# Ten of the twelve modulation tensors of a two-layer diffusion trunk, computed on GpSimd instead of TensorE

## The chip, the cores and the metric

The kernel runs on one core of one Trainium2 chip. Its time is the device time in microseconds of one execution; lower is better. TensorE multiplies matrices into PSUM, VectorE (DVE) and ScalarE (ACT) do elementwise work, GpSimd (POOL) is a fourth compute engine that this kernel hardly uses, and SyncE (SP) issues all DMAs from one queue, in order.

## The reference, cut to what matters

Two layers are applied to 128 context tokens and 512 latent tokens, with the same weights for both kinds. Each layer needs six modulation vectors of 1024 numbers for each kind of token: a shift, a scale and a gate for the mixer half, and the same for the ConvFFN half.

```python
def adaln(cvec, w, b):                       # w: (1024, 6 * 1024)
    m = jax.nn.silu(cvec) @ w + b
    return m.reshape(cvec.shape[0], 6, D_MODEL)

def trunk_layer(x, mod, lp, cache):
    sh_m, sc_m, gt_m, sh_f, sc_f, gt_f = [mod[:, i][:, None] for i in range(6)]
    h = rmsnorm(x, lp['norm_g'][0]) * (1 + sc_m) + sh_m
    ...                                      # three branches: GQA attention, S5, neighbourhood attention
    x = x + gt_m * rmsnorm(merged @ lp['w_out'], lp['norm_g'][1])
    h = rmsnorm(x, lp['norm_g'][2]) * (1 + sc_f) + sh_f
    f = conv_ffn(h, ...)
    return x + gt_f * rmsnorm(f, lp['norm_g'][3])
```

So twelve vectors in all (two layers by six), each the product of a 2x1024 matrix (one row for the context tokens, one for the latent ones) with a 1024x1024 block of w_mod. All data are float32.

## The kernel before, in words

The dense weights come as 308 chunks of 128x1024 floats (512 KB), 154 for each layer, in the order of their use. `ws_next` hands out one chunk: at each call it prepares the chunks up to two ahead (`ws_prep`: ScalarE rounds the raw chunk to `hi`, VectorE takes `lo = raw - hi`; both through helpers, lines L130 and L99) and issues the loads up to four ahead (`ws_load`, which keeps the last issue as `last_ws`). There are two raw buffers and three pairs of hi and lo. A dense product is three TensorE passes (hi by hi, hi by lo, lo by hi; all matmuls have line L227). A chunk of the dense kind is 48 matmuls on 640 tokens, in halves of 384 and 256.

The order in a layer: S5 input projection (zu, 4 chunks), S5 sums and scan, GQA projections (zq 4 and zkv 2), gates, GQA attention, S5 output and GLU, branch products, then the neighbourhood attention with its projections (nv 4; nq and nk for each of four head pairs) woven with the rest of the gates and branch products, then w_out (8 chunks, one of them loaded twice), the FFN's up-projection (44 chunks; conv and SiLU on VectorE and ScalarE), and w_down (22 chunks for three token tiles, and then for the other two tiles in reverse, three of them kept, so 41 loads). In layer 0's up-projection the S5 bases and taps of layer 1 (`s5_pre`: many products on VectorE) are woven in, one step for each chunk. The order of instructions on each engine is made when the program is built, by a scheduler that follows program order as priority (`top()` raises it) and a simulated clock; each engine then runs its list in order, and so does the DMA queue of SP.

Modulation vectors 0 and 1 of layer 0 are computed in `setup`. The other ten are computed by `adaln` (L466): vectors 2, 3 and 4 of layer 0 in the neighbourhood stage (woven in at 1.4 steps for each step of that stage, with one raw buffer, into PSUM bank m1), vector 5 of layer 0 and all six of layer 1 in layer 0's up-projection (two raw buffers, bank tq). One step loads 512 KB of w_mod and does four matmuls of 256 columns, one on each 32-column quarter of the array, with the conditioning vectors (padded to 32 columns, tile `scv`) as the stationary side:

```python
for q in range(4):
    self.mm(acc[32 * q:32 * q + 32, 0:256], self.scv[:, k, :], t[:, q * 256:q * 256 + 256],
            k == 0, k == 7)
yield
```

Eight steps make a vector, so the ten vectors are 80 steps. Shift and scale vectors are then turned into columns by two transposes (`mod_store`); the two gates of a layer are written to DRAM as rows, from where `out_phase` reads them.

Vector 2 of a layer is needed at the start of w_out, 3 and 4 in the norm that follows it, 5 at the start of w_down, and 0 and 1 of layer 1 in the norm after the first token tiles of layer 0's w_down.

In the neighbourhood stage, `na_proj` loads the cached keys (`ck2`) and the bias for each pair of heads into the tiles `set` and `sf`, of which there are two; the mask is loaded once.

Of the kernel before, what the change touches and what calls it, by code (L numbers as in the profile page):

```python
# [50 lines left out]
class Trunk:  # L51
# [112 lines left out]
    def ws_init(self):  # L164
        self.third = None
        self.n_load = self.n_prep = self.n_use = 0
        self.raw_t, self.hl_t = {}, {}
# [40 lines left out]
    def ws_next(self, *key):  # L208
# [6 lines left out]
        self.n_use += 1  # L215
        return self.hl_t.pop(i)
# [109 lines left out]
    def setup(self):  # L326
# [22 lines left out]
        self.scv = c.tile([128, 8, 32], F, name="scv")  # L349
        nc.vector.memset(self.scv.rearrange("p k m -> p (k m)"), 0.0)  # L350
        self.act(th, cc, AF.Tanh, scale=0.5)
        self.stt(th, th, 1.0, cc, ALU.add, ALU.mult)
        self.ts(self.scv[:, :, 0:2].rearrange("p k s -> p s k"), th.rearrange("p (s k) -> p s k", s=2), 0.5, ALU.mult)
        self.alloc_h()
        with ExitStack() as es:
            pool = self.pool(es, "start")
            wm = []
# [26 lines left out]
            def unit(i):  # L384
                acc = accs[i] = self.px() if i < 2 else self.ps()
                for k in range(8):
                    for q in range(4):
                        self.mm(acc[32 * q:32 * q + 32, 0:128], self.scv[:, k, :],
                                wm[i][:, k, q * 128:q * 128 + 128], k == 0, k == 7)
# [58 lines left out]
    def mod_columns(self, l, vec, acc, n, kb, pool):  # L448

        sb = pool.tile([128, 256], F, tag="ad", name="adsb")  # L450
        self.act(sb[:, :n], acc[:, :n])
        self.transpose(acc[:, 256:384], sb[:, :n])
# [13 lines left out]
    def adaln(self, l, vecs, pool, raw, bank):  # L466

        todo = [(v, k) for v in vecs for k in range(8)]
        raws = []

        def load():
            if todo:
                v, k = todo.pop(0)
                with self.top():
                    raws.append(raw(k))
                    self.dma(raws[-1], self.A["wmod"][l, v, k])

        load()
        for v in vecs:
            acc = bank()  # L480
            for k in range(8):
                load()
                t = raws.pop(0)
                for q in range(4):
                    self.mm(acc[32 * q:32 * q + 32, 0:256], self.scv[:, k, :], t[:, q * 256:q * 256 + 256],
                            k == 0, k == 7)
                yield
            for c in (0, 128):
                sb = pool.tile([128, 128], F, tag="ad", name="adsb")
                a = acc[:, c:c + 128]  # L490
                if v in (2, 5):
                    gb = pool.tile([128, 2, 128], F, tag="gb", name="gb")
# [1098 lines left out]
```

## Time and profile before

| | us |
|---|---|
| runs, median of 3 (lowest to highest) | 2423.01 (2422.66 to 2423.14) |
| profiled execution, device time | 2418.54 |
| profiled execution, span from first to last instruction | 2416.8 |
| TensorE matmul busy in the span | 2334.5 (97%) |
| TensorE weight load busy | 2103.6 (87%) |
| VectorE busy | 1501.8 (62%) |
| ScalarE busy | 1221.7 (51%) |
| GpSimd busy | 0.7 |
| granted TensorE clock, mean share of full speed | 0.99 |

The stages of layer 0 lie in the span about as follows: zq, zkv and the S5 scan from 140 to 225 us, GQA and the S5 output to 445, the neighbourhood stage to 673, w_out and its norm to 760, up-projection to 1130, w_down to 1280. Layer 1 has the rest: attention stages to 1660, neighbourhood to 1880, w_out to 1942, up-projection to 2255, w_down to the end. A busy share is an average over the stage; what limits a stage is read from the waits in it.

### The profile page before, as it was taken

The numbers are of one execution on the slowest core, as the hardware profiler recorded it, in microseconds if no ns is written. First come the engines' busy times: TensorE is split into PE (matmuls) and PEld (weight loads), VectorE is DVE, ScalarE is ACT, GpSimd is POOL, SyncE is SP. The second block draws the span as 40 slices with busy tenths as digits, with TensorE's granted clock in tenths as the row PEclk, the third lists the DMA queues.
The fourth block names the chain that finished last, engine by engine and source line by source line (L and its number), as shares of the span: only waits on it lengthen the run. The fifth ranks groups of instructions, "written<-read, shape, count | busy, mean of one in ns | idle before, by whom it ended". The sixth has DMA issues, their size and how long they took to land.

```text
span 2416.8 us, 41307 instructions
## 1 busy us (share of the span) xinstructions
PE 2334.5 (97%) x16026; PEld 2103.6 (87%) x16026; DVE 1501.8 (62%) x3339; ACT 1221.7 (51%) x2657; POOL 0.7 (0%) x6
## 2 busy tenths in 40 slices
PE   5999999998999999999999999999999999999998
PEld 4899898877887899999888998888998899999886
DVE  8789647366557776665474495463775665444456
ACT  5434676336536444344364447754474564444444
POOL 0000000000000000000000000000000000000000
PEclk8999999999999999999999999999999999999999
DMA  7863242444244666654555323413321532222335
GB/s 270 276 220 98 100 147 68 161 147 132 80 157 159 204 200 208 201 173 138 170 183 186 121 81 124 138 49 124 97 64 54 176 130 71 79 72 78 114 114 174
DMA packets 160270, 334.56 MB, mean 138 GB/s; under 512 B 39434, under 2 KB 73290, under 8 KB 160074
## 3 DMA queue, kind: packets, MB, share of 16 engines
q1 hardware_dynamic: 160074, 331.92, 41.7%
q8 instruction: 126, 2.06, 0.4%
q14 instruction: 70, 0.57, 0.1%
HBM read 288.71 MB, written 52.53 MB: 141 GB/s over the span
## 4 chain that ended last, share of the span: by engine, by line
PE 85%; DMA 4%; ACT 4%; DVE 3%; issue 1%; SPq 0%; DVEq 0%; ACTq 0%
PE mm L227 49%; PE m L227 16%; PE mx L227 7%; PE tq L227 4%; PE y L227 3%; PE PT L230 2%; DMA ar<-in_wmod 2%; PE sc L227 1%; DMA raw<-in_wst 1%; ACT HK L130 1%; DVE lo L99 1%; PE BT L230 1%; ACT h L130 1%; PE E L227 1%; DMA cd<-pr 1%
## 5 line engine op out<-in xcount | busy, mean ns | idle before, releaser
L227 PE MATMUL mm<-h,hi 128*128 128x384 f32 (+1 forms) x3808 | 855.8, 313 | 6.3 <-ACT h L130 4.1
L227 PEld LDWEIGHTS mm<-h,hi 128*128 128x128 f32 x3808 | 642.7, 190 | 23.4 <-issue 12.8
L227 PE MATMUL mm<-h,lo 128*128 128x384 f32 (+1 forms) x1904 | 593.7, 312 | 0.0
L99 DVE TENSOR_TENSOR lo<-raw,hi 128x1024 fp32r<-128x1024 f32 x294 | 359.6, 1224 | 294.2 <-ACT hi L130 282.6
L130 ACT ACTIVATE hi<-raw 128x1024 fp32r<-128x1024 f32 x294 | 310.9, 1058 | 291.5 <-PE mm L227 196.6
L227 PEld LDWEIGHTS mm<-h,lo 128*128 128x128 f32 x1904 | 361.5, 190 | 5.2 <-issue 4.9
L227 PE MATMUL m<-h,hi 128*128 128x256 f32 (+1 forms) x1120 | 250.6, 312 | 2.1 <-ACT vn L130 1.1
L227 PEld LDWEIGHTS m<-h,hi 128*128 128x128 f32 x1120 | 188.7, 190 | 7.8 <-issue 4.4
L227 PE MATMUL m<-h,lo 128*128 128x256 f32 (+1 forms) x560 | 174.0, 311 | 0.1
L117 DVE SCALAR_TENSOR_TENSOR c<-u,blob,c 128x641 f32<-128x641 f32 x156 | 137.9, 884 | 2.2
L130 ACT ACTIVATE PT<-PT 128x512 f32<-128x512 f32 (+1 forms) x176 | 86.8, 498 | 93.1 <-PE PT L230 72.9
L227 PEld LDWEIGHTS m<-h,lo 128*128 128x128 f32 x560 | 106.2, 190 | 1.8 <-issue 1.4
L130 ACT ACTIVATE u<-mm 128x256 f32<-128x256 f32 (+1 forms) x156 | 48.0, 344 | 117.0 <-PE mm L227 117.0
L227 PE MATMUL mm<-a,hi 128*128 128x384 f32 (+1 forms) x384 | 89.3, 320 | 4.2 <-ACT a L130 3.1
L130 ACT ACTIVATE HK<-a 64x32 f32<-64x32 f32 (+1 forms) x256 | 77.5, 337 | 8.2 <-PE mm L227 6.2
L227 PE MATMUL mm<-hi,sph 128*128 128x512 f32 x208 | 78.6, 393 | 1.5 <-ACT sph L130 1.4
L227 PE MATMUL mm<-lo,sph 128*128 128x512 f32 x208 | 78.5, 392 | 0.0
L99 DVE TENSOR_TENSOR pr<-PW,cS 128x576 f32<-128x576 f32 x64 | 47.9, 755 | 48.3 <-PE mx L227 32.3
L227 PE MATMUL mm<-set,hi 128*128 128x384 f32 (+1 forms) x324 | 74.8, 317 | 0.5 <-DVE a L117 0.4
L227 PE MATMUL mm<-hi,spl 128*128 128x512 f32 x208 | 73.2, 393 | 0.0
L130 ACT ACTIVATE c<-u,blob 128x641 f32<-128x641 f32 x78 | 72.2, 925 | 1.9
L227 PEld LDWEIGHTS mm<-a,hi 128*128 128x128 f32 x384 | 63.9, 190 | 7.5 <-ACT a L130 4.1
(357 smaller groups left out, 4295.3 us busy)
## 6 DMA issues: line engine op xcount, KB each, us to landing
raw<-in_wst SPq DMA_DIRECT2D x308, 512.0 KB, 3.7
ar<-in_wmod SPq DMA_DIRECT2D x80, 512.0 KB, 4.0
cd<-pr SPq DMA_DIRECT2D x32, 288.0 KB, 4.4
v<-cd SPq DMA_DIRECT2D x32, 288.0 KB
wm<-in_wmod SPq DMA_DIRECT2D x8, 1024.0 KB
xd<-xt SPq DMA_DIRECT2D x15, 512.0 KB, 2.8
xt<-xd SPq DMA_DIRECT2D x15, 512.0 KB, 6.0
bd<-BT SPq DMA_DIRECT2D x28, 256.0 KB, 3.7
```

The source lines that it names most:

```text
L99: return self.nc.vector.tensor_tensor(out=out, in0=a, in1=b, op=op)
L117: self.nc.vector.scalar_tensor_tensor(out=out, in0=a, scalar=s, in1=b, op0=op0, op1=op1)
L130: return self.nc.scalar.activation(out=out, in_=a, func=func, **kw)
L227: return self.nc.tensor.matmul(out=out, lhsT=lhsT, rhs=rhs, start=start, stop=stop)
L230: return self.nc.tensor.transpose(out, in_, self.ident)
```

## The change

The matmuls of `adaln` go, and so does its weaving into the neighbourhood stage and the up-projection. A generator, `modulation`, begins in layer 0 once the S5 scan has been written out, and `ws_next` advances it by one step for each chunk handed out. A step loads half a chunk of w_mod (128x512 floats, 256 KB, two buffers `mraw`), ordered on SP behind the last weight load, and issues GpSimd operations: for each kind of token a product with that token's conditioning number of each partition, and, from the second step of a half on, an addition to a running sum. Sixteen steps make a vector, eight for each half, so ten vectors are 160 steps. After each half, `mod_sum` (called three or four steps later) adds up the 128 partitions on TensorE: eight matmuls of 128 columns with a stationary tile of zeros and ones, into a bank of the pool `tp`, and then the columns or the gate rows as before. The rows of the gate constants (`gb`) are laid out for halves on the host.

To make room, the bias tile `sf` loses the cached keys, which go with the mask into a tile `nrest` that shares the two buffers of the softmax tile `P`; the mask is now loaded for every pair of heads. The neighbourhood stage of layer 0 no longer sets `apart`, so its projections use a third PSUM bank, as in layer 1. `setup` keeps `sc` (128x2x8) instead of the padded `scv`.

```diff
@@ ws_next
         self.n_use += 1
+        if self.mod is not None:
+            next(self.mod, None)
         return self.hl_t.pop(i)
@@ instead of adaln
+    def modulation(self):
+        nc, A, pool = self.nc, self.A, self.p_c
+        due = None
+        for l, v in [(0, v) for v in range(2, 6)] + [(1, v) for v in range(6)]:
+            for hf in range(2):
+                acc = pool.tile([128, 2, 512], F, tag="macc", name="macc", bufs=2)
+                for k in range(8):
+                    raw = pool.tile([128, 512], F, tag="mraw", name="mraw", bufs=2)
+                    with self.tc.issue_after(self.last_ws.ins):
+                        self.dma(raw, A["wmod"][l, v, k][:, hf * 512:hf * 512 + 512])
+                    for s in range(2):
+                        to = acc[:, s] if k == 0 else pool.tile([128, 512], F, tag="mtmp", name="mtmp")
+                        sc = self.sc[:, s, k:k + 1].to_broadcast([128, 512])
+                        nc.gpsimd.tensor_tensor(out=to, in0=raw, in1=sc, op=ALU.mult)
+                        if k:
+                            nc.gpsimd.tensor_tensor(out=acc[:, s], in0=acc[:, s], in1=to, op=ALU.add)
+                    if k == 3 and due:
+                        self.mod_sum(*due)
+                    yield
+                due = l, v, hf, acc
+        for _ in range(3):
+            yield
+        self.mod_sum(*due)
+    def mod_sum(self, l, v, hf, part):
+        if l not in self.blob:
+            self.load_blob(l)
+        pool, acc = self.p_c, self.tp("mod")
+        for s in range(2):
+            for q in range(4):
+                self.mm(acc[32 * q:32 * q + 32, 0:128], self.ones[:, s], part[:, s, q * 128:q * 128 + 128], s == 0, s == 1)
+        if v not in (2, 5):
+            self.mod_columns(l, v, acc, 128, slice(4 * hf, 4 * hf + 4), pool)
+            return
+        sb = pool.tile([128, 128], F, tag="ad", name="adsb")
+        gb = pool.tile([128, 512], F, tag="mraw", name="gb", bufs=2)[:, 0:256].rearrange("p (j c) -> p j c", j=2)
...
@@ mixer
                     self.dma(self.O["ssm"][l], HS[:, 16].rearrange("p r g -> p (r g)"))
+                    if l == 0:
+                        self.mod = self.modulation()
...
                 na = self.neighbourhood(l, p_na, p_y, self.Ga)
-                if l == 0:
-                    self.apart = True
-                    raw = lambda k: p_na.tile([128, 1024], F, tag="ar", name="ar", bufs=1)
-                    na = self.weave(na, self.adaln(0, (2, 3, 4), p_na, raw, self.m1), 1.4)
                 self.run_all(na)
-                self.apart = False
@@ na_proj
-        q, kk, bias, ck2, kc = ops
+        q, kk, bias, kc = ops
+        rest = pool.tile([128, 768], F, tag="P", name="nrest", bufs=2)
+        ck2 = rest[:, 512:768].rearrange("p (h k) -> p h k", h=2)
...
+                mask = rest[:, 0:512].rearrange("p (i k) -> p i k", i=2)
+                self.dma(mask, self.A["nmask"])
                 for hh in range(2):
-                    self.add(bias[:, hh], bias[:, hh], self.nmask)
+                    self.add(bias[:, hh], bias[:, hh], mask)
@@ ffn
-                mod = chain(self.adaln(l, (5,), p_mod, raw, self.tq), self.adaln(l + 1, range(6), p_mod, raw, self.tq))
-                for _ in range(16):
-                    next(mod)
-                up = self.weave(up, mod, 1.0)
```

## Rows read from the trace of the kernel before

**Rows 1.** The page: busy time by engine, and the chain that ended last.
```profile
PE 2334.5 (97%) x16026; PEld 2103.6 (87%) x16026; DVE 1501.8 (62%) x3339; ACT 1221.7 (51%) x2657; POOL 0.7 (0%) x6
PE 85%; DMA 4%; ACT 4%; DVE 3%; issue 1%; SPq 0%; DVEq 0%; ACTq 0%
```
**Rows 2.** Busy time by stage; columns: stretch, length, PE, PEld, DVE, ACT, POOL, clock, DMA.
```profile
140.00:225.00 85.00, 85.00 (x609) 81.45 (x609) 76.87 (x225) 35.74 (x79) 0.00 (x0) 1.00 0.48 149
445.00:673.00 228.00, 213.21 (x1487) 176.36 (x1485) 129.64 (x310) 112.81 (x296) 0.00 (x0) 0.98 0.38 125
673.00:760.00 87.00, 83.38 (x431) 71.69 (x432) 58.56 (x156) 39.70 (x74) 0.00 (x0) 1.00 0.41 146
760.00:860.00 100.00, 97.95 (x747) 83.90 (x746) 75.94 (x194) 47.35 (x93) 0.00 (x0) 1.00 0.66 219
860.00:1090.00 230.00, 230.00 (x1751) 213.90 (x1751) 150.09 (x229) 94.16 (x177) 0.00 (x0) 1.00 0.61 192
1090.00:1130.00 40.00, 40.00 (x284) 38.91 (x283) 19.68 (x27) 17.21 (x32) 0.00 (x0) 1.00 0.33 107
1130.00:1222.00 92.00, 92.00 (x405) 75.53 (x404) 45.83 (x62) 38.68 (x57) 0.00 (x0) 1.00 0.48 159
1222.00:1280.00 58.00, 58.00 (x267) 47.82 (x266) 45.91 (x88) 41.98 (x66) 0.00 (x0) 1.00 0.62 204
1660.00:1880.00 220.00, 216.22 (x1513) 198.06 (x1512) 144.04 (x334) 118.15 (x303) 0.00 (x0) 1.00 0.24 75
```
**Rows 3.** Timeline of TensorE, up-projection of layer 0: start, us, what.
```profile
920.28 0.64 PE L227 MATMUL tq<-ar,scv 128*32 128x256 f32 x8
920.85 0.66 PE L230 MATMUL BT<-ident,pr 128*128 128x128 f32 x4
```
**Rows 4.** Instruction groups, TensorE, 445 to 673 us: busy, mean ns, idle before.
```profile
L227 PE MATMUL m<-ar,scv 128*32 128x256 f32 x192 | 18.8, 400 | 6.6 <-DMA ar<-in_wmod 6.6
```
**Rows 5.** Timeline of TensorE in setup: matmuls of 128 columns with scv.
```profile
32.28 1.07 PE L227 MATMUL mm<-wm,scv 128*32 128x128 f32 x28
33.28 0.66 PE L230 MATMUL xT<-ident,a 128*128 128x128 f32 x4
```
**Rows 6.** Instruction groups of GpSimd, whole span.
```profile
masks.py:199 POOL TENSOR_SCALAR_AFFINE_SELECT ident<-ident 128x128 f32<-128x128 f32 x1 | 0.3, 292 | 0.1
masks.py:197 POOL MEMSET ident<- 128x128 f32 x1 | 0.2, 204 | 0.3 <-POOLq L1574 0.3
L1574 POOL MEMSET const-float32-1.0<- 128x1 f32 x1 | 0.1, 98 | 0.0
```
**Rows 7.** Instruction groups of VectorE, 860 to 1090 us.
```profile
L117 DVE SCALAR_TENSOR_TENSOR c<-u,blob,c 128x641 f32<-128x641 f32 x56 | 49.3, 881 | 0.2
L99 DVE TENSOR_TENSOR lo<-raw,hi 128x1024 fp32r<-128x1024 f32 x28 | 34.1, 1219 | 6.9 <-ACT hi L130 6.9
L99 DVE TENSOR_TENSOR pr<-PW,cS 128x576 f32<-128x576 f32 x32 | 24.2, 755 | 37.5 <-PE mx L227 32.3 <-PE BT L230 5.2
L99 DVE TENSOR_TENSOR pr<-PW,bS 128x512 f32<-128x512 f32 x19 | 13.0, 688 | 19.1 <-PE BT L230 19.1
```
**Rows 8.** Weight loads issued in 140:225, 673:760, 760:860, 1130:1222 and 1222:1280, in order.
```profile
raw<-in_wst SPq DMA_DIRECT2D x10, 512.0 KB, 4.3
...
raw<-in_wst SPq DMA_DIRECT2D x12, 512.0 KB, 3.5
...
raw<-in_wst SPq DMA_DIRECT2D x11, 512.0 KB, 6.6
...
raw<-in_wst SPq DMA_DIRECT2D x22, 512.0 KB, 3.6
...
raw<-in_wst SPq DMA_DIRECT2D x18, 512.0 KB, 3.7
```
**Rows 9.** Weight and modulation loads issued in 860:1090, and weight loads in 1090:1130.
```profile
ar<-in_wmod SPq DMA_DIRECT2D x30, 512.0 KB, 4.0
raw<-in_wst SPq DMA_DIRECT2D x28, 512.0 KB, 4.4
...
raw<-in_wst SPq DMA_DIRECT2D x6, 512.0 KB
```
**Rows 10.** The chain of waits at 1733 us: start, us, what.
```profile
1733.49 4.88 DMA sf<-in_cknt
```

More of the change, by code (lines that the diff above doesn't have):

```diff
@@ L1 @@
 from contextlib import ExitStack
-from itertools import chain
 import numpy as np
@@ L356, in setup @@
             pool = self.pool(es, "start")
+            scv = pool.tile([128, 8, 32], F, tag="scv", name="scv")
+            self.memset(scv.rearrange("p k m -> p (k m)"), 0.0)
+            self.cpy(scv[:, :, 0:2].rearrange("p k s -> p s k"), self.sc)
             wm = []
@@ L464, in mod_store @@
             self.mul(dst, dst, col(B_NG + 8 * (0 if vec == 1 else 2)))
[L466 to L492, printed above, removed]
-                    self.dma(gb, self.A["gb"][l, v // 3][:, :, c:c + 128])
-                    self.add(sb, a, gb[:, 0])
-                    self.mul(sb, sb, gb[:, 1])
-                    for s in range(2):
-                        row = self.ggd[l][v // 3][s].rearrange("o (q c) -> (o q) c", q=4)
-                        self.dma(row[:, c:c + 128], sb[s::32, :])
-                else:
-                    self.act(sb, a)
-                    self.transpose(acc[:, 256 + c:384 + c], sb)
-            if v not in (2, 5):
-                self.mod_store(l, v, acc, 256, slice(0, 8))
@@ new lines, in mod_sum @@
+    def mod_sum(self, l, v, hf, part):
[8 more added lines that the diff above has]
+            return
+        sb = pool.tile([128, 128], F, tag="ad", name="adsb")
+        gb = pool.tile([128, 512], F, tag="mraw", name="gb", bufs=2)[:, 0:256].rearrange("p (j c) -> p j c", j=2)
+        self.dma(gb, self.A["gb"][l, v // 3][:, :, hf * 128:hf * 128 + 128])
+        self.add(sb, acc[:, 0:128], gb[:, 0])
+        self.mul(sb, sb, gb[:, 1])
+        for s in range(2):
+            row = self.ggd[l][v // 3][s].rearrange("o (h q c) -> h (o q) c", h=2, q=4)
+            self.dma(row[hf], sb[s::32, :])
@@ L1387, in ffn @@
         blob = self.blob[l]
-        if l + 1 < NL:
+        if l + 1 < NL and l + 1 not in self.blob:
             with self.tc.issue_after(self.first.ins):
@@ L1404, in ffn @@
             up = self.up_phase(l, f, us, p_u, blob, ahead)
+            for _ in range(ahead):
+                next(up)
+            self.es_skew.close()
+            ft.append(self.slot_v())
             if l + 1 < NL:
-                raw = lambda k: p_mod.tile([128, 1024], F, tag=f"ar{k % 2}", name="ar")
-                mod = chain(self.adaln(l, (5,), p_mod, raw, self.tq), self.adaln(l + 1, range(6), p_mod, raw, self.tq))
-                for _ in range(16):
-                    next(mod)
-                up = self.weave(up, mod, 1.0)
-                for _ in range(ahead):
-                    next(up)
-                self.es_skew.close()
-                ft.append(self.slot_v())
-                up = self.weave(up, self.s5_pre(l + 1, es, self.px), 1.0)
-            else:
-                for _ in range(ahead):
-                    next(up)
-                self.es_skew.close()
-                ft.append(self.slot_v())
+                up = self.weave(up, self.s5_pre(l + 1, es, self.px), 1.0)
             self.run_all(up)
```

35 lines of the change are left out of this document (16 added, 19 removed).

## The prediction

> **What bounds the kernel now.** First the page: matmuls are busy for 97% of the span and 85% of the chain that ended last is TensorE, so time is won by taking work from TensorE, as long as nothing else becomes late [rows 1]. Then busy time by stage, which shows what stands close behind TensorE. In layer 0 VectorE is at 76.9 of 85 us beside the projections and the S5 scan, 58.6 of 87 in w_out, 75.9 of 100 and 150.1 of 230 in the up-projection, 45.9 of 58 in the second part of w_down; GpSimd has nothing to do anywhere [rows 2]. Last the groups of VectorE in the up-projection: nearly all its time there goes to operations that read two tensors from SBUF (lo, the convolution, the S5 products) [rows 7]. The reader is to see that the change moves work from an engine at its limit to an idle one, in stages where the engine next in line is itself at 50 to 90%.
>
> **What is removed.** 80 steps of four matmuls. Each matmul shows as two records, eight for a step; from the start of a step's first record to the next instruction it is 0.57 us [rows 3], so 80 x 0.57 = 45.6 us of TensorE. In the neighbourhood stage, with one raw buffer, TensorE also waited 6.6 us for these loads [rows 4]. Together 52 us. As a check: that stage has 14.8 us of idle TensorE in layer 0 and 3.8 in layer 1, which has no modulation [rows 2].
>
> **What is added on TensorE.** 20 calls of mod_sum with eight matmuls of 128 columns, 16 records each. In setup, 28 such records take 1.00 us from their start to the next instruction [rows 5], 0.036 us each: 16 x 0.036 = 0.57, so 20 x 0.6 = 12 us. The transposes stay twelve. The result of a half is asked for three or four chunks after its last product was issued; in dense stages that is over 20 us, so I cost that wait at nothing where GpSimd keeps up. Net gain of TensorE: 52 - 12 = 40 us.
>
> **What is added on GpSimd.** 160 steps; two products each and two additions in seven of eight: 3.75 operations of 128x512 a step, 600 in all. The trace has no such operation. Lower bound: VectorE's two-input operation of that size, 0.69 us [rows 7]. Upper bound: GpSimd's only operation with an input takes 292 ns for 128 elements, of which 98 are fixed, so 1.52 ns an element; twice that for two inputs gives 98 + 2 x 1.52 x 512 = 1.65 us [rows 6]. Between them: a memset costs (204 - 98)/128 = 0.83 ns an element, so the input is worth 0.69; a second one makes 2.2 ns an element and 98 + 2.2 x 512 = 1.2 us, which I take as nearest to GpSimd's own rows. A step is then 3.75 x 1.2 = 4.5 us, all of them 720 us.
>
> The Trainium skill ("GPSIMD Engine Reference", section on elementwise cycle accounting) gives 4497 ns for a two-input operation on 2048 floats; a quarter is 1.12 us, an estimate, and a step would be 4.2 us. No run here shows it yet.
>
> 4.5 us fits in a dense chunk: 28 loads in 230 us are 8.2 us each [rows 2, 9]. It doesn't fit in w_down's second part, 58 us for 18 loads or 3.2 us each [rows 2, 8]. There it matters that GpSimd's loads wait in SP's queue: with two buffers, the load of a step waits until the products of two steps before are done, and behind it wait all later weight loads, and so lo, hi and TensorE. GpSimd can't fall far behind without stopping TensorE, unless the order made at build time already placed its loads late.
>
> **What the two elementwise engines do to each other.** Nothing in the trace shows GpSimd and VectorE at work on SBUF together, so I bound it from both sides. Low end: they run side by side, and nothing is added while VectorE plus TensorE fit as they do. High end: an operation of VectorE with two SBUF inputs and an operation of GpSimd take turns, and a stage lasts at least the sum of both. I take the high end for stages where VectorE is mostly on such operations; the sums, with 4.5 us for each weight load [rows 2, 8, 9]:
> - 140 to 225: VectorE 76.9, less about 12 for reductions and PSUM sources, 65 + 10 x 4.5 = 110, against 85: +25.
> - 673 to 760: 58.6 less about 14 from PSUM, 44 + 12 x 4.5 = 98, against 87: +11.
> - 760 to 860: about 70 + 11 x 4.5 = 120, against 100: +20.
> - 860 to 1090: 150 + 28 x 4.5 = 276, against 230: +46.
> - 1090 to 1130: 20 + 6 x 4.5 = 47, against 40: +7.
>
> That is +109, and TensorE's saving in these stages (56 of the 80 steps) is swallowed. In w_down, 92 + 40 x 4.5 = 272 against 150: +122 if the loads keep step with the chunks, 0 if they are placed late and their work falls into layer 1's first stages, which have room. I take a quarter, +30, because 4.5 us against 92/22 = 4.2 and 3.2 us a chunk makes any order that knows GpSimd's pace let it trail. In the neighbourhood stage VectorE has 130 of 228, so there the gain stays: 24 x 0.57 + 6.6 = 20; mod_sum takes 5 of it back there and in GQA. Sum: 109 + 30 - 20 + 5 = +124.
>
> The Trainium skill ("SBUF — State Buffer", "Who interferes with whom") says that a VectorE instruction with two SBUF inputs contends with a GpSimd instruction that reads SBUF, and that the second to issue fully blocks until the first is done. By that rule the high end holds, and moving work between these two engines buys little; without it the low end would, and the time would be that of the first rival. This trace can't show it.
>
> **Smaller edits.** The loads of w_mod keep their bytes (160 x 256 KB for 80 x 512 KB); the mask is loaded eight times. The cached keys now wait for a softmax buffer before their load can start. In layer 1 that load already stood on the chain for 4.88 us [rows 10]. Three pairs in each layer follow another pair, so from 0 to 6 x 4.9 = 29 us; I take 0, since projections and gates lie beside most of them, and keep 29 for the range. The bank that m1 gives back in layer 0 only helps and is in the 20 us above.
>
> **The forecast.** The profiled 2418.5 + 124 = 2542.5; the median of the runs lies 4.5 above the profiled execution (2423.0 - 2418.5), so 2547 us, 5% slower. Its own range is 2450 (half the turns hidden by prepared weights) to 2640 (w_down pays its 122).
>
> **The rivals.**
> 1. Side by side: the engines don't hinder each other and the 40 us of TensorE come through: 2423 - 40 = 2383; with w_down paced by GpSimd, 18 x 4.5 = 81 against 58, up to 2406. For it: TensorE's 97%, and GpSimd's 4.5 us within 8.2. Against it: two engines streaming SBUF where VectorE has no slack. It decides from the point where VectorE's two-input operations keep their 0.69 and 1.22 us beside GpSimd.
> 2. A slower GpSimd: 1.65 us an operation, 6.2 a step. The five sums become 127, 118, 138, 324 and 57, +222 in all; w_down a quarter of (92 + 40 x 6.2 - 150), +48; less 15: +255, 2678 us. For it: the only GpSimd row with an input is slow.
> 3. The neighbourhood stage gives the gain back: rival 1 with 29 us for keys and mask behind the softmax buffers: 2412, and with w_down's 23 us 2435. For it: [rows 10]; against it: only one such wait stands on the chain there now.
>
> That the change doesn't do what it says (work still on TensorE) is excluded by the code.
>
> **How the numbers follow.** Forecast 0.50, rival 1 0.31, rival 2 0.10, rival 3 0.09. This kernel's runs can tell about 0.2%, 5 us, from no change. Faster by more than that: rival 1 and 0.02 of rival 3, 0.33. Within: 0.06 of rival 3. Slower: the rest, 0.61. The range for 8 in 10 must hold both signs: from 2380, just under rival 1, to 2640, the forecast's upper end; left out are most of rival 2 and a little below rival 1.
>
> **What would show it.** Right: GpSimd operations of about 1.2 us alone; VectorE's lo well above 1.22 us, or gaps before it with no releaser, while GpSimd is busy; TensorE idle from 860 on behind lo; the up-projection of layer 0 longer, that of layer 1 at 313 us as before. Wrong: lo still at 1.22 us, TensorE without gaps, and a period of 7.6 us a chunk (8.2 less 0.57) in the up-projection; or a loss that sits in w_down alone (the queue), or in the neighbourhood stage of both layers (the shared buffers).

## The result: 6.3% slower, 2576 us

| | before | after |
|---|---|---|
| runs, median (lowest to highest) | 2423.07 (2422.66 to 2424.4) | 2576.41 (2575.59 to 2578.81) |
| span of the profiled execution | 2416.8 | 2574.7 |
| TensorE idle in the span (neither matmul nor weight load) | 61.0 | 192.0 |
| granted TensorE clock, mean | 0.990 | 0.969 |

The ratio is 1.0633, with a 95% interval of 1.0615 to 1.0652. Lines of the kernel after lie one or two off those of before (matmuls have L228, `lo` L98).

The page's busy times and its chain, which answer to [rows 1]:
```profile
PE 2361.5 (92%) x15706; PEld 2138.6 (83%) x15706; DVE 1861.8 (72%) x3355; ACT 1216.6 (47%) x2657; POOL 867.9 (34%) x606
PE 44%; DVE 18%; issue 4%; ACT 3%; POOL 2%; DMA 2%; SPq 0%; DVEq 0%; ACTq 0%; POOLq 0%
```
VectorE has sixteen instructions more and is busy for 360 us more. TensorE has 320 records fewer and is busy for 27 us more. On the chain VectorE went from 3% to 18%, and GpSimd itself has only 2%: it does its harm through another engine.

The stages while GpSimd works, which answer to [rows 2] (stretch, length, then busy time of PE, PEld, DVE, ACT and POOL, clock, DMA):
```profile
140.00:242.00 102.00, 88.26 (x645) 82.93 (x641) 98.72 (x183) 36.18 (x90) 55.20 (x36) 0.95 0.48 150
489.00:683.00 194.00, 178.13 (x1207) 159.96 (x1206) 156.59 (x260) 94.03 (x246) 170.13 (x131) 0.97 0.41 134
683.00:788.00 105.00, 87.07 (x483) 70.12 (x484) 86.95 (x152) 38.35 (x92) 59.39 (x42) 0.97 0.36 120
788.00:920.00 132.00, 108.33 (x664) 103.38 (x663) 113.95 (x223) 60.60 (x114) 59.98 (x43) 0.91 0.31 101
920.00:1165.00 245.00, 218.78 (x1549) 210.70 (x1548) 237.12 (x243) 91.09 (x177) 159.45 (x99) 0.97 0.45 146
1212.00:1311.00 99.00, 88.71 (x386) 67.68 (x385) 72.26 (x48) 32.32 (x44) 92.19 (x62) 0.97 0.56 184
1311.00:1393.00 82.00, 63.51 (x274) 47.53 (x272) 76.39 (x85) 40.59 (x73) 71.67 (x49) 0.90 0.51 171
1393.00:1530.00 137.00, 114.31 (x829) 97.49 (x829) 83.14 (x113) 48.04 (x127) 112.83 (x87) 0.91 0.53 173
```
In the S5 scan (first row) and in the up-projection (fifth) VectorE is busy for 97% of the stretch, where it had 90% and 65%. It has become the bound there. In w_down and the first stages of layer 1 (the last three rows) GpSimd is at 82 to 93%.

The instruction groups behind it, which answer to [rows 7] and give what [rows 6] could not:
```profile
L98 DVE TENSOR_TENSOR lo<-raw,hi 128x1024 fp32r<-128x1024 f32 x294 | 431.3, 1468 | 230.0 <-ACT hi L129 227.1
L116 DVE SCALAR_TENSOR_TENSOR c<-u,blob,c 128x641 f32<-128x641 f32 x156 | 170.6, 1093 | 2.0
L490 POOL TENSOR_TENSOR mtmp<-mraw,sc 128x512 f32<-128x512 f32 x280 | 375.0, 1339 | 289.1 <-DMA mraw<-in_wmod 271.7
L492 POOL TENSOR_TENSOR macc<-macc,mtmp 128x512 f32<-128x512 f32 x280 | 440.6, 1574 | 21.2
L490 POOL TENSOR_TENSOR macc<-mraw,sc 128x512 f32<-128x512 f32 x40 | 52.2, 1325 | 349.6 <-PE mod L228 216.4
```
These means mix two kinds of time. Sorted by what lies beside them, `lo` takes 1.225 us (median of 183) with no GpSimd operation beside it and 2.06 us (median of 77) with GpSimd busy for at least 95% of its time; the convolution's `c` 0.886 and 1.69. GpSimd's product takes 1.04 us alone and its sum 1.29 (medians of 18 and 21). The last row holds a surprise: for 216 us, in GQA, GpSimd stood and waited for a `mod_sum` that came late in TensorE's order. A long stretch in which VectorE wasn't at its limit (152.7 of 247 us) went by nearly unused.

How the two engines look together, in the timeline of the up-projection (start, length, what); VectorE first, then GpSimd:
```profile
999.82 1.52 DVE L98 TENSOR_TENSOR pr<-PW,bS 128x512 f32<-128x512 f32 x1
1001.27 2.32 DVE L98 TENSOR_TENSOR lo<-raw,hi 128x1024 fp32r<-128x1024 f32 x1
1003.51 1.53 DVE L98 TENSOR_TENSOR pr<-pr,pr 128x512 f32<-128x512 f32 x1
1004.96 1.92 DVE L116 SCALAR_TENSOR_TENSOR c<-u,blob,c 128x641 f32<-128x641 f32 x1
```
```profile
999.22 1.57 POOL L490 TENSOR_TENSOR mtmp<-mraw,sc 128x512 f32<-128x512 f32 x1
1000.87 1.63 POOL L492 TENSOR_TENSOR macc<-macc,mtmp 128x512 f32<-128x512 f32 x1
1002.58 1.91 POOL L490 TENSOR_TENSOR mtmp<-mraw,sc 128x512 f32<-128x512 f32 x1
1004.56 1.63 POOL L492 TENSOR_TENSOR macc<-macc,mtmp 128x512 f32<-128x512 f32 x1
```
Neither engine has a gap of note: both look fully busy, and they do half and two thirds of what they could. Alone, the four operations of VectorE take 0.69 + 1.22 + 0.69 + 0.88 = 3.48 us and the four of GpSimd 2 x (1.04 + 1.29) = 4.66, together 8.1. Here each set takes 7.0 us. So the waiting isn't seen as idle time: it is inside the durations, where a comparison of means with the trace of before shows it.

The lines also show the turns one by one. `lo` starts while GpSimd's sum (from 1000.87 us) is running, and ends 1.09 us after it (1003.59 against 1002.50): nearly the 1.22 us that it needs alone, as if it had started when the sum was done. The next product starts at 1002.58, beside `lo`, and ends 0.90 us after it, of the 1.04 that it needs alone. So it is in the whole trace: 89 `lo` began while a product or a sum was running; 82 of them ended 1.08 us after it (1.079 to 1.088), however much of it was left. Of the other 7, which took 1.21 to 1.23 us, 4 had at most 0.13 us of the operation left, and 3 met one that itself took 2.3 to 4.3 us. The `c` that waited, 35 of them, ended 0.68 us after GpSimd's operation.

**Where the time went, stage by stage.** The table gives the time between the issues of two weight loads (the 308 loads come in the same order in all kernels), so that a stage is the same work in each. A load is issued some chunks before its use, and part of a difference can stand one stage earlier or later; sums over neighbours don't move. e1 is the first experiment below: the change with next to nothing on GpSimd.

| loads (stage) | before | e1 | after | after - before | forecast |
|---|---|---|---|---|---|
| 0 to 13 (setup, zu) | 113.5 | 109.9 | 117.0 | +3.5 | 0 |
| 13 to 24 (projections, scan) | 87.7 | 90.0 | 115.2 | +27.5 | +25 |
| 24 to 61 (GQA to neighbourhood) | 452.0 | 429.0 | 450.2 | -1.8 | -15 |
| 61 to 73 (w_out) | 81.4 | 81.2 | 100.7 | +19.3 | +11 |
| 73 to 84 (norm, up-projection begins) | 104.4 | 87.5 | 118.3 | +13.9 | +20 |
| 84 to 118 (up-projection) | 267.7 | 251.6 | 283.7 | +16.0 | +53 |
| 118 to 156 (w_down) | 140.1 | 151.9 | 188.5 | +48.4 | +30 |
| 156 to 168 (layer 1: zu to zkv, S5 sums) | 100.9 | 103.8 | 132.4 | +31.5 | 0 |
| 168 to 307 (rest) | 1016.7 | 1016.8 | 1015.8 | -0.9 | 0 |
| sum | | | | +157.4 | +124 |

### The profile page after: what moved, and what is told of

It is laid out like the page before. It is cut to its first block, busy times and chain, and to the rows that moved or that the text cites. A ratio compares the mean times of both kernels' runs of the same rounds, so it can differ in the third digit from the quotient of the medians.

```text
span 2574.7 us, 41611 instructions
## 1 busy us (share of the span) xinstructions
PE 2361.5 (92%) x15706; PEld 2138.6 (83%) x15706; DVE 1861.8 (72%) x3355; ACT 1216.6 (47%) x2657; POOL 867.9 (34%) x606
## 3 DMA queue, kind: packets, MB, share of 16 engines
q8 instruction: 124, 2.03, 0.3%
## 4 chain that ended last, share of the span: by engine, by line
PE 44%; DVE 18%; issue 4%; ACT 3%; POOL 2%; DMA 2%; SPq 0%; DVEq 0%; ACTq 0%; POOLq 0%
PE mm L228 24%; PE m L228 10%; PE mx L228 4%; DVE lo L98 3%; DVE c L116 3%; DVE pr L98 3%; PE y L228 2%; PE tq L228 1%; PE PT L231 1%; POOL macc L492 1%; POOL mtmp L490 1%; DVE a L98 1%; ACT HK L129 1%; DVE spl L98 1%; DMA raw<-in_wst 1%
## 5 line engine op out<-in xcount | busy, mean ns | idle before, releaser
L228 PE MATMUL mm<-h,hi 128*128 128x256 f32 (+1 forms) x3696 | 842.7, 316 | 32.4 <-ACT u L129 13.6
L228 PEld LDWEIGHTS mm<-h,hi 128*128 128x128 f32 x3696 | 635.6, 193 | 41.6 <-ACT u L129 15.1
L98 DVE TENSOR_TENSOR lo<-raw,hi 128x1024 fp32r<-128x1024 f32 x294 | 431.3, 1468 | 230.0 <-ACT hi L129 227.1
L228 PE MATMUL mm<-h,lo 128*128 128x256 f32 (+1 forms) x1848 | 582.7, 315 | 0.0
L490 POOL TENSOR_TENSOR mtmp<-mraw,sc 128x512 f32<-128x512 f32 x280 | 375.0, 1339 | 289.1 <-DMA mraw<-in_wmod 271.7
L492 POOL TENSOR_TENSOR macc<-macc,mtmp 128x512 f32<-128x512 f32 x280 | 440.6, 1574 | 21.2
L228 PEld LDWEIGHTS mm<-h,lo 128*128 128x128 f32 x1848 | 356.9, 193 | 2.6 <-issue 2.5
L228 PE MATMUL m<-h,hi 128*128 128x256 f32 (+1 forms) x1232 | 277.8, 314 | 9.2 <-ACT u L129 7.5
L228 PEld LDWEIGHTS m<-h,hi 128*128 128x128 f32 x1232 | 210.0, 192 | 13.2 <-ACT u L129 8.5
L228 PE MATMUL m<-h,lo 128*128 128x256 f32 (+1 forms) x616 | 192.3, 312 | 0.1
L116 DVE SCALAR_TENSOR_TENSOR c<-u,blob,c 128x641 f32<-128x641 f32 x156 | 170.6, 1093 | 2.0
L490 POOL TENSOR_TENSOR macc<-mraw,sc 128x512 f32<-128x512 f32 x40 | 52.2, 1325 | 349.6 <-PE mod L228 216.4
L228 PEld LDWEIGHTS m<-h,lo 128*128 128x128 f32 x616 | 118.3, 192 | 0.8 <-DVE lo L98 0.4
L129 ACT ACTIVATE c<-c 128x641 f32<-128x641 f32 x44 | 32.6, 741 | 160.8 <-DVE c L116 160.8
L228 PE MATMUL mm<-a,hi 128*128 128x256 f32 (+1 forms) x384 | 89.5, 321 | 2.4 <-ACT a L129 1.7
L228 PE MATMUL mm<-hi,spl 128*128 128x512 f32 x208 | 76.6, 411 | 14.9 <-DVE spl L98 13.8
L228 PE MATMUL mm<-hi,sph 128*128 128x512 f32 x208 | 81.0, 403 | 3.8 <-ACT sph L129 3.8
L228 PE MATMUL mm<-lo,sph 128*128 128x512 f32 x208 | 81.7, 407 | 2.9 <-DVE lo L98 2.7
L98 DVE TENSOR_TENSOR a<-a,sx 128x64 f32<-128x64 f32 (+1 forms) x256 | 78.7, 307 | 7.3 <-ACT a L129 4.9
```

Source lines behind the costliest of these rows:

```text
L98: return self.nc.vector.tensor_tensor(out=out, in0=a, in1=b, op=op)
L116: self.nc.vector.scalar_tensor_tensor(out=out, in0=a, scalar=s, in1=b, op0=op0, op1=op1)
L129: return self.nc.scalar.activation(out=out, in_=a, func=func, **kw)
L228: return self.nc.tensor.matmul(out=out, lhsT=lhsT, rhs=rhs, start=start, stop=stop)
L490: nc.gpsimd.tensor_tensor(out=to, in0=raw, in1=sc, op=ALU.mult)
L492: nc.gpsimd.tensor_tensor(out=acc[:, s], in0=acc[:, s], in1=to, op=ALU.add)
```

## The experiments

All are compared with the kernel before in the same job (2422.4 to 2424.2 us). A diff is against the kernel after unless it says otherwise.

**e1: the change with next to no work on GpSimd.** Theory T is that GpSimd's reads and VectorE's two-input operations take turns. The rival puts the loss on the moved loads, `mod_sum` or the order. Ten modulation vectors are left out but for eight columns of each half; the running sums are set to zero first.

```diff
...
-    nc.gpsimd.tensor_tensor(out=to, in0=raw, in1=sc, op=ALU.mult)
+    nc.gpsimd.tensor_tensor(out=to, in0=raw[:, 0:8], in1=sc, op=ALU.mult)
...
-    nc.gpsimd.tensor_tensor(out=acc[:, s], in0=acc[:, s], in1=to, op=ALU.add)
+    nc.gpsimd.tensor_tensor(out=acc[:, s, 0:8], in0=acc[:, s, 0:8], in1=to, op=ALU.add)
```


> The changed kernel, but each GpSimd product and sum covers 8 of the 512 columns (the running sums are set to zero first; the modulation is left out but for those columns). Loads, waits, the order of the queue, mod_sum and the moved keys and mask stay. Theory T (VectorE operations with two SBUF inputs, and those in its fast one-input mode, take turns with GpSimd operations that read SBUF): the loss goes, 2383 to 2410 us, lo back at 1.22 us. Rival Q (the load of half a chunk stands in SP's queue until GpSimd is done, and the weight loads behind it are late): GpSimd is never late, so also 2383 to 2410. Rival O (moved keys, mask, mod_sum and another instruction order cost the time): stays above 2450.

Measured: 2377.76 us (2376.17 to 2378.69), ratio 0.9813 (0.9794 to 0.9833). Its busy times and its `lo`:
```profile
PE 2298.8 (97%) x15706; PEld 2099.9 (88%) x15706; DVE 1503.5 (63%) x3355; ACT 1221.1 (51%) x2657; POOL 221.1 (9%) x626
L98 DVE TENSOR_TENSOR lo<-raw,hi 128x1024 fp32r<-128x1024 f32 x294 | 359.7, 1224 | 289.5 <-ACT hi L129 279.4 <-DMA bts<-bd 6.6 <-DMA cd<-pr 1.1
```
The loads, `mod_sum`, the order and the moved keys and masks are all there, and the kernel is 45 us faster than before, though GpSimd's short operations still take 221 us. So TensorE's relief is real, and all of the loss, 199 us from here to the kernel after, comes with GpSimd's work. The loads and `mod_sum` aren't free: in w_down and the stage after it (loads 118 to 168) e1 is 14.7 us slower than before, and it makes up for that elsewhere. It splits in two by the busy lines and the idle times: TensorE idle 55 against 192 us (+137), and TensorE busy 2298.8 against 2361.5 (+63) for the same 15706 records. Most of the second part is the clock. It was granted at 0.989 in e1 and at 0.969 after; over the time in which TensorE was busy, the share that wasn't granted adds up to 18 us in e1 and to 63 in the kernel after, 45 us more. What makes the other 18 isn't shown. The windows around layer 0's norm in the kernel after show how it comes about:
```profile
812.00:824.00 12.00, 12.00 (x70) 12.00 (x69) 10.25 (x17) 1.61 (x3) 9.49 (x8) 1.00 0.48 156
824.00:836.00 12.00, 6.58 (x37) 6.26 (x36) 7.39 (x14) 6.10 (x14) 7.09 (x5) 0.86 0.28 99
836.00:848.00 12.00, 12.00 (x90) 11.55 (x89) 6.54 (x22) 6.51 (x14) 0.00 (x0) 0.85 0.01 2
848.00:860.00 12.00, 12.00 (x94) 12.00 (x94) 11.66 (x27) 9.35 (x15) 0.73 (x1) 1.00 0.47 154
```
TensorE stood for half of the second row, and the clock fell; in the third it is at work all the time, and a mean of 0.85 (some of it at 1.2 GHz, the rest at 2.4) says that it paid for the gap after the gap was over.

**e2: GpSimd as busy, but writing instead of reading.** 1200 memsets of 128x512 take the place of the products and sums, beside the eight columns of e1.

```diff
+    for _ in range(2 if k == 0 else 4):
+        nc.gpsimd.memset(tmp, 0.0)
```


> As e1, with memsets of 128x512 in front of each small product, two in the first step of a half and four in the others for each kind of token, so that GpSimd is busy about as long as in the changed kernel (a memset of that size should take 0.5 us; a step about 4.5 us) but reads next to nothing. Theory T: reads are what VectorE's second input collides with, so lo stays near 1.22 us and the time near e1's, at most 2420 us. Rival Q: GpSimd's pace is the same as in the changed kernel, so the loads are as late: 2540 to 2580 us.

Measured: 2432.64 us (2426.24 to 2437.22), ratio 1.0043 (1.0024 to 1.0061). GpSimd's memsets, VectorE's `lo` and TensorE's `mod_sum`:
```profile
L491 POOL MEMSET mtmp<- 128x512 f32 x1200 | 635.9, 530 | 67.9
L98 DVE TENSOR_TENSOR lo<-raw,hi 128x1024 fp32r<-128x1024 f32 x294 | 359.6, 1224 | 295.5 <-ACT hi L129 291.3 <-DMA cd<-pr 1.1 <-PE tp L231 0.9
L228 PE MATMUL mod<-macc,ones 128*32 128x128 f32 x320 | 16.3, 294 | 33.2 <-POOL macc L496 32.9
```
GpSimd was busy for 883.5 us, as much as in the kernel after (867.9), and `lo` kept its 1.22 us throughout. A busy GpSimd doesn't slow VectorE; one that reads does. This is what separates the two, and it agrees with the rule weighed in the prediction (the Trainium skill, "SBUF — State Buffer", "Who interferes with whom"): a GpSimd instruction that only writes doesn't contend with a two-input instruction of VectorE. But T had expected at most 2420 us, and the kernel lost 55 us on e1. TensorE waited 33 us in `mod_sum` for sums that weren't ready, and the stage of loads 156 to 168 took 137.8 us, against 103.8 in e1. So there is a second cause, GpSimd's pace, which VectorE has no part in.

From e1 to after that makes 55 us of pace and 144 us of collision, as far as the two can be told apart. The 55 are rather too many: e2's GpSimd is as busy as the one that collisions have slowed, while the same operations alone would take 160 x 4.3 = 690 us.

**e3: no steps in w_down and in layer 1's first stages.**
```diff
-        if self.mod is not None:
+        if self.mod is not None and not (key[0] == "w_down" or key[:2] in (("zu", 1), ("zq", 1), ("zkv", 1))):
```


> The changed kernel, but no modulation step is taken while chunks of w_down of layer 0 and of zu, zq and zkv of layer 1 are handed out; the steps left go on in layer 1's attention stages. The whole computation is done. Theory T: the loss of w_down and of layer 1's first stage (48 and 31 us between the weight loads 118, 156 and 168) goes, and some comes back in layer 1, where VectorE has room: 2490 to 2530 us. Rival Q: much the same, since w_down's short chunks are where GpSimd is late. Rival O: no change, 2576.

Measured: 2550.37 us (2549.62 to 2551.23), ratio 1.0526 (1.0506 to 1.0547). The two stages came back whole: 139.9 us from load 118 to 156 and 101.3 to 168, as before the change. Those 80 us came with the steps in stages that had no room for them; e1, which has the steps without GpSimd's work, is 14.7 us slower there, so some 65 are the work itself. But the gain is 26 us and not 46 to 86: the steps left over fell into layer 1, where loads 168 to 215 took 52 us longer than in the kernel after (537.2 against 484.8). The loss moves with the work.

**e4: half the vectors back on TensorE.** GpSimd has vectors 2, 3 and 4 of each layer, the steps beginning at each layer's scan; vector 5 of layer 0, and 0, 1 and 5 of layer 1, are computed by the old `adaln` in the up-projection.
```diff
-        for l, v in [(0, v) for v in range(2, 6)] + [(1, v) for v in range(6)]:
+        for v in (2, 3, 4):
...
-                    if l == 0:
-                        self.mod = self.modulation()
...
+                    self.mod = self.modulation(l)
...
+                mod = chain(self.adaln(l, (5,), p_mod, raw, self.tq), self.adaln(l + 1, (0, 1, 5), p_mod, raw, self.tq))
```


> A version meant to be faster than both: GpSimd only makes vectors 2, 3 and 4 of each layer, one half chunk for each chunk from the gates on (attention and neighbourhood stages, VectorE at 55 to 65%); vector 5 of layer 0 and 0, 1 and 5 of layer 1 stay on TensorE in layer 0's up-projection, as before the change. The whole computation is done. Theory T: 48 TensorE steps of 0.57 us and 6.6 us of waits go, 12 calls of mod_sum cost 7 us, and the stages have room for both engines: 2395 to 2415 us. Rival O (moved keys and mask): 2425 to 2450.

Measured: 2484.35 us (2482.51 to 2485.65), ratio 1.0256 (1.0231 to 1.028). The expectation was too low by 70 to 90 us. I had thought of GQA and the neighbourhood as free. But the loads of `mraw` ran ahead in the order made at build time, and GpSimd worked beside the S5 scan of layer 0 (+22.6 us) and beside the gates of layer 1 (loads 168 to 178, 106.9 us against 79.8). With 493 us of GpSimd, VectorE was busy for 168 us more than before.

**e5: the same sums on VectorE itself.** One operation does product and sum:
```diff
-    nc.gpsimd.tensor_tensor(out=to, in0=raw, in1=sc, op=ALU.mult)
...
-    nc.gpsimd.tensor_tensor(out=acc[:, s], in0=acc[:, s], in1=to, op=ALU.add)
+    self.stt(acc[:, s], raw, self.sc[:, s, k:k + 1], acc[:, s], ALU.mult, ALU.add)
```
(and `self.ts` with ALU.mult for the first step of a half).

> The changed kernel with the same sums on VectorE: per step and kind of token one operation (raw times the conditioning number plus the running sum) of 128x512, about 0.69 us, so 160 x 2 x 0.69 = 220 us more of VectorE and nothing on GpSimd. The whole computation is done. Theory T (VectorE and GpSimd exclude each other): VectorE grew by 360 us in the changed kernel (1501.8 to 1861.8) through waiting alone, so doing the work itself is cheaper: 2385 to 2440 us. A rival (VectorE has no room for any of it in the projections, w_out and the up-projection, whoever does it): above 2500 us.

Measured: 2424.1 us (2420.73 to 2426.97), ratio 1.0003 (0.9993 to 1.0013): the time of before. Its busy times, and its new operation (shortest, median, longest duration in ns, first and last start):
```profile
PE 2316.1 (96%) x15706; PEld 2110.2 (87%) x15706; DVE 1691.1 (70%) x3675; ACT 1224.9 (51%) x2657; POOL 0.7 (0%) x6
L116 DVE SCALAR_TENSOR_TENSOR macc<-mraw,sc,macc x280: 734/746/810, 100.4 to 1379.8; 128x512 f32<-128x512 f32 x140
```
This is the sharpest result of the study. VectorE does the whole job in 1691.1 - 1501.8 = 189 us. With the job on GpSimd it loses 360 us to waiting, and the kernel 152 us more. Handing work to an idle engine cost VectorE nearly twice what doing the work costs it. GpSimd does it in two operations where VectorE has one; whether a single operation on GpSimd would halve the harm wasn't tried.

**e6: e2 with `mod_sum` four steps later**, to see whether e2's loss was TensorE standing in `mod_sum`, or SP's queue. (Against e2.)
```diff
-                    if k == 3 and due:
+                    if k == 7 and due:
```


> As e2 (GpSimd busy with memsets, hardly reading; the modulation is left out but for 8 columns), but mod_sum is called four steps later, in the eighth step of the next half. If e2's 55 us over e1 are TensorE standing in mod_sum until GpSimd's last sum (33 us of idle TensorE in e2's trace end there), this falls to 2380 to 2405 us. If they are late weight loads behind half chunks in SP's queue, it stays at 2425 to 2440.

Measured: 2413.79 us (2405.67 to 2419.74), ratio 0.9964 (0.995 to 0.9978): between the two. TensorE's wait in `mod_sum` fell from 32.9 to 9.4 us, and 19 of the 55 us came back. Its idle time ahead of `mod_sum` in e6 (us, times):
```profile
  POOL macc L496: 9.4, 3
```
The other 36 weren't traced to one wait, but the loads show where they lie. By load 168 e6 is 19 us behind e1, where e2 was 56 behind; then it loses 29 us in layer 1's gates and GQA (loads 168 to 188: 254.6 us against 225.4 in e1 and 224.2 in e2) and wins 9 back later. So here too a part of the loss moved. What SP's queue can do is seen in the kernel after, in the issues of SP around 1312 us:
```profile
1307.78 0.86 SPq L135 DMA_DIRECT2D raw<-in_wst  x2
1312.59 16.27 SPq L135 DMA_DIRECT2D mraw<-in_wmod  x4
1328.95 0.38 SPq L135 DMA_DIRECT2D raw<-in_wst  x1
```
Four loads of half chunks held the queue for 16 us, with two buffers whose content GpSimd has yet to read, and the next weight load stood behind them.

**e7: the product with a scalar for each partition**, so that it reads one tensor instead of two.
```diff
-    sc = self.sc[:, s, k:k + 1].to_broadcast([128, 512])
-    nc.gpsimd.tensor_tensor(out=to, in0=raw, in1=sc, op=ALU.mult)
+    nc.gpsimd.tensor_scalar(out=to, in0=raw, scalar1=self.sc[:, s, k:k + 1], scalar2=None, op0=ALU.mult)
```


> The changed kernel with the product as an operation of one tensor and a number per partition instead of two tensors (the second a broadcast). The whole computation is done. By GpSimd's own row of one input (1.52 ns an element) the product would take 0.88 us alone instead of 1.04. Theory T: the loss goes with GpSimd's reading time, so 153 us shrink by about 320 x 0.16 = 51 us of 740: 2555 to 2570 us. If only two-input operations of GpSimd hindered VectorE, half the operations would be harmless: below 2510.

Measured: 2556.95 us (2551.06 to 2560.39), ratio 1.0555 (1.0531 to 1.0578). That lies where T put it, but not for its reason. The groups of GpSimd's product and of `mod_sum`:
```profile
L489 POOL TENSOR_SCALAR mtmp<-mraw,sc 128x512 f32<-128x512 f32 x280 | 571.7, 2042 | 131.1 <-DMA mraw<-in_wmod 107.2
L228 PE MATMUL mod<-macc,ones 128*32 128x128 f32 x320 | 17.2, 306 | 74.8 <-POOL macc L491 74.8
```
Beside this product alone `lo` keeps its 1.21 us (median of 32), and where a sum follows the product during it 1.23 (median of 48); where it meets a sum first and then a product, it takes 2.03 (median of 31). So VectorE was hindered less (busy for 1728.5 us against 1861.8), though not left alone: of 48 `c` that began during such a product, 30 took 1.2 us or more. But the one-input product takes 1.56 us alone, half as long again as the two-input one (1.04), and 2.04 on the mean: here it is GpSimd that waits. It fell behind, and TensorE stood 75 us in `mod_sum`.

**e8 and e9: one pace, two engines.** Both have two steps for each chunk in layer 0's neighbourhood stage, and none in the S5 scan, the gates, w_down and layer 1's first stages. e8 computes as e5, e9 as the kernel after.
```diff
         if self.mod is not None:
-            next(self.mod, None)
+            rate = 2 if 36 <= i < 58 else int(28 <= i < 36 or 69 <= i < 117 or i >= 164)
+            for _ in range(rate):
+                next(self.mod, None)
```


> The sums on VectorE, as in e5 (one operation of 128x512 for each step and kind of token, 0.75 us), but with the steps placed where VectorE has room: one step for each chunk in GQA's second half and the up-projection of layer 0, two for each in its neighbourhood stage, none in w_down and in the first stages of layer 1, one for each chunk from layer 1's gates on. Theory T (e5 lost its 40 us of TensorE where VectorE was already the bound: 28 us in gates and GQA of layer 0, 21 us from zu to the gates of layer 1): both stages come back to e1's times, and the doubled rate adds at most 20 us of VectorE's in the neighbourhood stage; 2385 to 2410, faster than before by 0.5 to 1.6%. Rival (any 190 us more on VectorE come out of the end somewhere, since TensorE and VectorE are both close to their limit): 2415 to 2435.

> The change as it was (products and sums on GpSimd), with the same pace as e8: two steps for each chunk in the neighbourhood stage of layer 0, none in the S5 scan, w_down and the first stages of layer 1. Theory T (it is the collision of two-input VectorE operations with GpSimd's reads, wherever it is placed): VectorE's busy time is again about 300 us above before, and most of it lies beside stages where VectorE or TensorE is at its limit; 2480 to 2560, and 80 us or more above e8. Rival (it was the place of the steps, above all the S5 scan and w_down): 2400 to 2440, within 30 us of e8.

Measured: e8 2418.37 us (2413.68 to 2420.55), ratio 0.9982 (0.9972 to 0.9991); e9 2532.99 us (2524.19 to 2535.2), ratio 1.0449 (1.0429 to 1.0469). The busy lines of e8 and of e9:
```profile
PE 2310.7 (96%) x15706; PEld 2109.7 (87%) x15706; DVE 1689.0 (70%) x3675; ACT 1219.9 (51%) x2657; POOL 0.7 (0%) x6
```
```profile
PE 2345.0 (93%) x15706; PEld 2129.0 (84%) x15706; DVE 1832.7 (72%) x3355; ACT 1215.2 (48%) x2657; POOL 842.1 (33%) x606
```
With the same calls in the same places, GpSimd costs 115 us more than VectorE. e9's rival, that only the place was wrong, is refuted: it had 2400 to 2440. For e8 the theory held in layer 0 (at load 178 it was 48 us ahead of before, and 5 ahead of e1) and failed in layer 1: by load 205 it was 29 us behind e1.

**e10 and e11: a third buffer for the half chunks**, in e8 and in e5. VectorE's idle time in e8 ahead of the first operation on a load (us, times):
```profile
  DMA mraw<-in_wmod: 85.7, 68
```
```diff
-    raw = pool.tile([128, 512], F, tag="mraw", name="mraw", bufs=2)
+    raw = pool.tile([128, 512], F, tag="mraw", name="mraw", bufs=3)
```


> e8 (sums on VectorE, paced) with three buffers for the half chunks of w_mod in place of two; the third takes the room of the product tile, which this version doesn't need. In e8 VectorE stood idle for 85.7 us, 68 times, until such a load had landed. Theory V (those waits hold up lo and the softmax behind them, and they are where e8's 34 us in the gates of layer 1 went): at least half of the 85.7 us goes, and the time is 2385 to 2408, faster than before by over 0.6%. Rival (VectorE's idle time before those loads cost nothing, since it had no other work then): 2412 to 2422, the same as e8.

> e5 (sums on VectorE, one step for each chunk from the S5 scan on) with three buffers for the half chunks. In e5 VectorE stood idle for 108.8 us, 71 times, until such a load had landed. Theory V: half of the losses in gates and GQA of layer 0 (28 us) and in the first stages of layer 1 (21 us) goes; 2395 to 2412. Rival (VectorE was full there): 2420 to 2428, the same as e5.

Measured: e10 2421.66 us (2417.4 to 2429.77), ratio 0.9994 (0.9982 to 1.0006); e11 2429.94 us (2428.05 to 2433.39), ratio 1.0024 (1.0014 to 1.0035). Theory V fell in both: the third buffer took only 11 of the 85.7 us (74.3 are left) and 4 of the 108.8 (105.0 are left), and nothing was won. This doesn't show what those waits cost, since most of them stayed.

**e12: layer 1's steps moved to its neighbourhood stage.** (Against e8.)
```diff
-            rate = 2 if 36 <= i < 58 else int(28 <= i < 36 or 69 <= i < 117 or i >= 164)
+            rate = 2 if 36 <= i < 58 or 188 <= i < 218 else int(28 <= i < 36 or 69 <= i < 117 or i >= 218)
```


> e8 (sums on VectorE, paced) with layer 1's part of the steps moved out of its gates, GQA and S5 output: none there, two for each chunk in its neighbourhood stage and the first chunks of w_out. At the weight load 178 e8 was 48 us ahead of the kernel before and 5 us ahead of e1; from there to load 205 TensorE's idle time was 23.0 us against 6.9 in e1, and it lost 29 us on e1. Theory P (the place decides: VectorE's sums cost little in the neighbourhood stage and much beside the gates and GQA): the 29 us come back but for about 10 to 15 in the neighbourhood stage, as the doubled rate cost in layer 0 (206.3 us against 196.7); 2385 to 2405, faster than before by 0.7% or more. Rival (the order made at build time shifts the loss to wherever the steps go): 2412 to 2422.

Measured: 2415.04 us (2411.09 to 2419.58), ratio 0.9966 (0.9955 to 0.9977), the best version that computes everything, 0.34% faster than before. The gates and GQA of layer 1 came back to e1's times (loads 168 to 195: 293.2 us against 292.1), as theory P said. But its neighbourhood stage (195 to 215) took 223.7 us against 193.9, a loss of 30 where 10 to 15 were allowed for, so the rival's range was met. No pace tried has room for all of VectorE's 189 us; e12 keeps 9 of the 45 us that e1 showed to be there.

## Why the prediction was right, and where its sum was off

The forecast, turns between VectorE and GpSimd, was the mechanism: e2 shows that it is GpSimd's reads, the times at which `lo` ends show the turns, and e1 shows that the rest of the change, taken together, gains time. 2576 lies 29 us above the 2547 predicted and inside the forecast's own 2450 to 2640. But the sum is better than its terms, and that is luck: the up-projection was put 37 us too high, GQA to neighbourhood 13 too low, and w_down with the stage behind it 50 too low.

- **What is removed: held.** 40 us net were forecast; e1 gained 45. Matmuls and waits together were read right [rows 3, 4]; the two were not measured apart.
- **GpSimd's operation: held.** 1.2 us were taken between 0.69 and 1.65; it is 1.04 for the product and 1.29 for the sum, so a step is 2 x 1.04 + 1.75 x 1.29 = 4.3 us, not 4.5. The estimate from the Trainium skill ("GPSIMD Engine Reference", section on elementwise cycle accounting), 1.12 us an operation, lies between the two. Rival 2 falls with it.
- **Side by side (rival 1): refuted** by the point given for it. `lo` didn't keep its 1.22 us.
- **The S5 scan: held.** +25 forecast, +27.5 measured. The sum of both engines' work is about the stage: 65 us of VectorE by the forecast's count and 36 operations of GpSimd at 1.16 us make 107, in a stretch of 102.
- **GQA to neighbourhood: too hopeful by 13.** A gain of 15 was forecast, because VectorE has 130 of 228 us there, and 1.8 came. In e1 the gain is 23. In e2, where VectorE keeps its times, it is 5.2: so GpSimd's pace alone can take most of it, and the forecast had put that at nothing.
- **w_out and the norm behind it: held together.** 11 + 20 forecast, 19.3 + 13.9 measured.
- **The up-projection: too much by 37.** 53 were forecast and 16 measured. I added the whole of VectorE's 150 us to 28 steps of 4.5 us and got 276 us. The stretch of 245 us has 99 operations of GpSimd, 115 us at 1.16 each, so the sum is 265 [rows 2, 7]. And a turn is a little shorter than the operation: `lo` ends 1.08 us after the operation that it waited for, and takes 1.22 alone, so 0.14 us of the two overlap. For 99 operations that would be 14 us, an estimate, and 251 are left. Some VectorE operations don't take turns at all, but the up-projection has next to none of them: reductions (the softmax's `mx<-Pn` of 128x384 takes 0.545 us alone and 0.544 beside GpSimd), reciprocals and operations that read PSUM.
- **w_down and what follows: too little by 50.** 30 were forecast; w_down lost 48.4 and layer 1's first stage, put at nothing, 31.5. The text had 122 for the case that the work keeps step with the chunks and took a quarter. The measured 80 are two thirds. The step that failed is "their work falls into layer 1's first stages, which have room": they had none. e3 shows both stages come back when the steps are taken away, and the work then cost 52 us in the later stages of layer 1. Nor did the work trail as far as was assumed: 113 of GpSimd's operations, 30 steps of the 40, started between loads 118 and 156, and 82 more by load 168. How much of this lateness comes from the 216 us in GQA in which GpSimd waited for `mod_sum` wasn't tried.
- **`mod_sum` at nothing: too low, a little.** TensorE waited for GpSimd's sums 10.8 us in the kernel after, and 32.9 us in e2. "Where GpSimd keeps up" was the condition, and it didn't.
- **The clock: not in the sum.** Of e1's distance to the kernel after, 63 us are TensorE's longer busy time, and 45 of these are clock that wasn't granted. The sums priced the turns alone; that TensorE also works slower behind an idle stretch (0.85 in the row from 836 us) stood nowhere in them.
- **Keys and masks at nothing (rival 3): held.** Loads 24 to 61 are 23 us shorter in e1 than before with all these loads in place, and those of layer 1's neighbourhood stage unchanged (193.9 against 193.6).
- **What would show it.** TensorE's idle time was foreseen behind `lo`. It is mostly behind ScalarE and VectorE operations one step later in the chain: 22.8 us behind ScalarE's `u`, 20.1 behind its `cp`, 15.0 behind VectorE's `pr`. `lo` is hardly among the releasers, so that sign failed, though its longer duration held.

What stays open: how the 36 us of pace that e6 left divide between SP's queue and the order made at build time; what the 18 us of TensorE's busy time are that the clock doesn't explain; and why in e12 the doubled rate costs 30 us in layer 1's neighbourhood stage, and in e8 only 10 in layer 0's, with as many operations in it (80 and 84).

## What to carry to other kernels

An idle engine isn't free if its work makes a busy one wait. Before work goes to GpSimd, list what VectorE does in that stage: where it is on two-input operations from SBUF and GpSimd would run two-input operations of this kind, add the two engines' times as if they were one engine (here that came out right in the S5 scan and 8% too long in the up-projection), and compare with VectorE doing the work itself in its fused form. And read the means of the untouched operations first in a trace: waiting that stands inside an instruction's duration appears in no view of idle time.

## What the runs showed that I had not expected

- GpSimd's one-input product with a scalar for each partition takes 1.56 us for 128x512; its two-input product with a broadcast operand takes 1.04 (e7).
- VectorE's one-input `Pn<-Pn,rc` of 128x384 in the softmax also stretched, from 0.42 us to as much as 1.54 beside GpSimd. The rule of two inputs would have left it out; the same section of the Trainium skill counts the one-input operations that run in a fast two-port mode among those that contend, and the trace agrees as far as this group goes: alone it takes 0.42 us, where the two-input `m<-m,a` of the same size takes 0.56.
- A GpSimd memset of 128x512 takes 0.53 us, and 1200 of them left VectorE's two-input operations at their times (e2).
